# A hybrid decoder layer on one core: the input on two queues, the first modulation on TensorE, the second shift and gate on GpSimd beside sparse attention

## The chip, the cores and the metric

The kernel runs on one core of a Trainium2 chip. The metric is the device time of one execution in microseconds (us); it is given as the median of three runs. The core's engines are TensorE (PE in the rows; PEld is its weight load), VectorE (DVE), ScalarE (ACT), GpSimd (POOL) and SyncE (SP). Each takes its own stream of instructions in the order in which it stands. SyncE and ScalarE issue most of the transfers here.

## What is computed

One layer over 1024 tokens of width 1024, float32. The reference, cut to what matters for the change:

```python
mod = c_act @ w_ada[l] + b_ada[l]
sh1, sc1, ga1, sh2, sc2, ga2 = [m[:, None, :] for m in jnp.split(mod, 6, axis=-1)]
h = rmsnorm(x, g_attn[l]) * (1.0 + sc1) + sh1
proj = h @ w_in[l]
qa, ka, va, qb, ckv, qi, ki, wi = jnp.split(proj, offsets, axis=-1)
out_a = dilated_mixture(...)
ckv = rmsnorm(ckv, kv_norm_g[l])
o_lat = sparse_attention(qi.reshape(bsz, seq, IDX_HEADS, IDX_DIM), ki, wi * IDX_SCALE, q_lat, ckv, slopes_b)
out_b = jnp.einsum('bthr,hrd->bthd', o_lat, w_uv[l])
x = x + ga1 * (mixed @ w_out[l])
h2 = rmsnorm(x, g_ffn[l]) * (1.0 + sc2) + sh2
gate, up = jnp.split(h2 @ w_gu[l], 2, axis=-1)
x = x + ga2 * ((jax.nn.silu(gate) * up) @ w_down[l])
return rmsnorm(x, g_final)
```

`c_act` is one row of 1024 numbers, the silu of `c`. `w_ada` is 1024 x 6144, so that the modulation is six products of a row with a 1024 x 1024 matrix, 25 MB of weights read once. Shift 1 and scale 1 (parts 0 and 1) are needed at once, gate 1 (part 2) by w_out, scale 2 and shift 2 (parts 4 and 3) by the feed-forward's norm, gate 2 (part 5) by its last product. The keys of group B are the 256 that an indexer scores highest; that search needs the scores of all keys of a block of queries.

## The kernel before

The kernel is one program; a scheduler puts each engine's instructions into an order worked out from a simulated timeline, with the program's order as priority. Only the matmuls of the attention stages are put in a fixed order by hand (`on_pe`, L761). Results of TensorE lie in tiles with the tags `mm`, `tp` and `o`; a tag has a few buffers that are taken in turn, so that a new tile of a tag waits until the one that had its buffer has been read.

*Start.* `load_x` (L105) fetches x in two halves of four tiles of 128 tokens. Each half comes as four pieces of 32 rows (`for r in (0, 2, 1, 3)`: each piece has the tokens of one remainder by 4), 512 KB, all eight on SyncE's queue (L252). Then the weights of two index projections (`wraw`, L209) and of the first modulation follow on it (`mod1_load`, L271: 2.1 MB for each of four groups of 256 columns of shift 1 and scale 1, into `va` and `score`, which aren't in use yet). ScalarE's queue meanwhile fetches the small tensors `cc` (this is `c`) and `gst`. `norm_half` (L254) squares and scales the rows. `mod1(g)` (L277) sums one group: VectorE multiplies eight slices of weights by the column `cc[:, k]` and adds them up in `macc` (L283, L285), TensorE then sums over the partitions (L289), and the sums go into the columns `a1`, `s1`. `h_part` (L297) transposes x, applies scale and shift and splits h into a high and a low float32r part, `hh` and `hl`: every projection is three matmuls of such parts (`mm3`, L367 to L369).

*Index stretch.* `qi_proj` makes the index queries, `latent` the latent keys and the index keys, and `idx_score` (L407) for each head the products of queries and keys (TensorE, L377), a relu (ScalarE, L419), and the weighted sum (VectorE, L425). `modulation` (L328) is a generator. A step of it sums 512 columns of parts 2, 4, 3 or 5: four loads of 512 KB into `va` (L339, SyncE), eight products of TensorE with 32 columns of `cz`, in which `c` stands padded with zeros (L342), a copy, and the sum over rows (L347 for the gates, one matmul of 512 columns; L351 for the columns of `a2` and `s2`, four matmuls of one column). `mod(4)` (L472) puts four of the eight steps in front of the index scores in the program's order; the rest come in the next stage.

*Search and group A.* VectorE finds each block's top keys by bisection (`score<-...`, L622), while TensorE does the other projections; then comes group A's attention.

*Group B.* Four passes, p = 0 to 3, of two heads each. A pass has six rounds of queries, and `staged` (L732) interleaves three steps of them: `scores(r)` (kB, qB; `mm`), `turn(r)` of the round before (transposition of the softmax numerators ttB; `tp`), and `values(r)` two rounds back (`o`). The first `scores` of a pass calls `pre_b(p)` (L1036): it loads the next pass's queries (`qraw`) and has GpSimd split them into qB (L512, L513), makes the latent keys of the next pass, and in pass 1 has GpSimd multiply half of w_out by gate 1 and split it (`wo_split`, L1011: L1015, L1019, L1020, four of each on 1024 columns). The scheduler starts these splits early, in pass 0.

*After B.* x is fetched again for the residual in 32 pieces of 128 KB (L110, by `load_x` from L1089); `mixed` (L1074) loads the attention's results (`mr`), and w_out follows in two halves of four heads' pairs. Then the feed-forward, with products combined so that seven take the place of eight, follows to the end.

## Time and profile before

| | |
|---|---|
| median of 3 runs | 1443.3 us (1442.92 to 1443.64) |
| the profiled execution | 1440.91 us |
| its span in the trace | 1439.1 us |
| mean granted clock of TensorE | 0.966 |
| TensorE busy | 1290.5 us, 90% of the span |
| VectorE busy | 1055.3 us, 73% |
| ScalarE busy | 592.5 us, 41% |
| GpSimd busy | 607.6 us, 42% |
| moved by DMA | 151.58 MB, 105 GB/s on average |

The profile is of one execution. Its span runs from the first to the last instruction seen; the execution's own time is 1.8 us more, and 2.4 us under the median of the three runs. "Busy" counts the time in which an engine works on an instruction; that of issuing a transfer isn't counted. In a group of instructions the name before the arrow is written, those behind it are read; the time after "idle before" is that in which the engine stood before them, and behind it stands what it waited for.

### The profile page before, as it was taken

What the parts mean: (1) busy time and instruction counts of PE and PEld (TensorE: products, weight loads), DVE (VectorE), ACT (ScalarE), POOL (GpSimd) and SP (SyncE); (2) the same over time, 40 slices, a digit from 0 to 9 for tenths busy, and PEclk for the clock granted to TensorE, in tenths of its full rate; (3) what the DMA queues carried; (4) which work ended last, traced back from release to release, by engine and by line L of the source; (5) the groups of instructions that cost most, each with busy time, mean ns of one, the idle gap of its engine ahead of it and who ended that gap; (6) DMA issues with size and microseconds to landing.
All of it is one profiled execution on the core that took longest, in us unless ns stands there. A gap on an engine that the chain in (4) does not pass through costs nothing.

```text
span 1439.1 us, 20308 instructions
## 1 busy us (share of the span) xinstructions
PE 1290.5 (90%) x7477; PEld 1030.0 (72%) x7477; DVE 1055.3 (73%) x1808; ACT 592.5 (41%) x1203; POOL 607.6 (42%) x386
## 2 busy tenths in 40 slices
PE   0798998999978999999869999999999998988894
PEld 0675576799766777778748888888888886766773
DVE  5926699999979576745999545555545469999897
ACT  2434446564255666622653333333333223223334
POOL 2641213132243062020576544445544436487865
PEclk9999999999989999999979999999999999999998
DMA  9724523425322220353523222222223291404004
GB/s 244 217 59 149 187 89 100 142 66 132 97 80 68 67 96 16 113 160 124 168 74 102 88 88 87 67 82 87 74 88 96 91 327 36 154 22 154 0 0 117
DMA packets 132477, 151.58 MB, mean 105 GB/s; under 512 B 9429, under 2 KB 95254, under 8 KB 132378
## 3 DMA queue, kind: packets, MB, share of 16 engines
q1 hardware_dynamic: 126416, 133.23, 30.4%
q0 software_dynamic: 4672, 15.73, 3.1%
q10 hardware_dynamic: 1290, 1.32, 0.3%
q8 instruction: 59, 0.97, 0.3%
q14 instruction: 40, 0.33, 0.1%
HBM read 115.13 MB, written 34.60 MB: 104 GB/s over the span
## 4 chain that ended last, share of the span: by engine, by line
PE 56%; DVE 28%; POOL 4%; issue 4%; DMA 3%; ACT 3%; SPq 1%; DVEq 0%; ACTq 0%; POOLq 0%
DVE score L622 7%; PE mm L1220 6%; PE mm L1218 6%; PE mm L1219 6%; PE mm L367 4%; PE mm L369 4%; PE mm L368 4%; PE o L764 3%; PE mm L764 3%; PE tp L1218 3%; PE tp L1220 3%; PE tp L1219 3%; PE tp L764 2%; DVE yacc L1338 2%; DVE wo L1328 2%
## 5 line engine op out<-in xcount | busy, mean ns | idle before, releaser
L1202 ACT ACTIVATE wo<-f 128x512 fp32r<-128x512 f32 x124 | 77.8, 630 | 174.2 <-PE mm L1220 77.4
L1203 DVE TENSOR_TENSOR wo<-f,wo 128x512 fp32r<-128x512 f32 x124 | 108.3, 876 | 39.1 <-ACT wo L1202 37.2
L367 PE MATMUL mm<-hh,wl 128*128 128x512 f32 (+2 forms) x288 | 112.3, 391 | 0.1
L368 PE MATMUL mm<-hh,wh 128*128 128x512 f32 (+2 forms) x288 | 110.6, 385 | 0.0
L369 PE MATMUL mm<-hl,wh 128*128 128x512 f32 (+2 forms) x288 | 109.7, 390 | 0.0
L214 POOL TENSOR_SCALAR wh<-wraw 128x1024 fp32r<-128x1024 f32 (+1 forms) x20 | 21.2, 1078 | 116.0 <-PE mm L369 65.4
L367 PE MATMUL mm<-wo,wo 128*128 128x512 f32 x148 | 59.4, 401 | 8.1 <-DVE wo L1328 8.1
L367 PEld LDWEIGHTS mm<-hh,wl 128*128 128x128 f32 (+1 forms) x288 | 54.8, 190 | 13.9 <-issue 1.7
L369 PEld LDWEIGHTS mm<-hl,wh 128*128 128x128 f32 (+1 forms) x288 | 53.5, 189 | 15.1 <-issue 4.2
L215 POOL TENSOR_TENSOR wl<-wraw,wh 128x1024 fp32r<-128x1024 f32 (+1 forms) x22 | 53.1, 2435 | 23.7 <-ACT wh L212 23.7
L368 PEld LDWEIGHTS mm<-hh,wh 128*128 128x128 f32 (+1 forms) x288 | 54.7, 190 | 11.7 <-issue 1.1
L1015 POOL TENSOR_TENSOR wor<-wor,ga 128x1024 f32<-128x1024 f32 x8 | 19.5, 2448 | 96.2 <-DMA wor<-in_w_out_dram 94.3
L369 PE MATMUL mm<-wo,wo 128*128 128x512 f32 x148 | 57.4, 397 | 1.4 <-DVE wo L1328 1.4
L368 PE MATMUL mm<-wo,wo 128*128 128x512 f32 x148 | 58.6, 396 | 0.0
L425 DVE SCALAR_TENSOR_TENSOR score<-rl,wi,score 128x384 f32<-128x384 f32 (+2 forms) x70 | 49.7, 750 | 7.2 <-ACT rl L419 4.6
L795 ACT ACTIVATE ttB<-ttB,mn 128x128 f32<-128x128 f32 (+7 forms) x64 | 49.1, 768 | 13.6 <-DVE mn L791 13.0
L1328 DVE TENSOR_TENSOR wo<-f,wo 128x1536 fp32r<-128x1536 f32 (+1 forms) x17 | 53.6, 3155 | 0.5 <-ACT wo L1327 0.5
L1272 POOL TENSOR_TENSOR f<-f 128x512 f32<-128x512 f32 x15 | 19.4, 1293 | 79.3 <-ACT f L1271 79.3
L367 PE MATMUL mm<-wo,ml 128*128 128x512 f32 x128 | 50.7, 396 | 2.0 <-DVE ml L1079 2.0
L622 DVE TENSOR_SCALAR_CACHE_REDUCE score<-ka,sc 128x768 bf16<-128x768 int16 (+2 forms) x48 | 52.3, 1140 | 0.0
L622 DVE TENSOR_SCALAR_CACHE_REDUCE score<-kl,sc 128x1024 bf16<-128x1024 uint16 (+2 forms) x48 | 52.3, 1140 | 0.0
L369 PE MATMUL mm<-wo,mh 128*128 128x512 f32 x128 | 50.4, 393 | 0.0
(453 smaller groups left out, 4196.6 us busy)
## 6 DMA issues: line engine op xcount, KB each, us to landing
f<-in_w_gu_dram SPq DMA_DIRECT2D x44, 512.0 KB, 3.9
va<-in_w_ada_dram SPq DMA_DIRECT2D x32, 512.0 KB, 4.7
spg<-f POOLq DMA_DIRECT2D x44, 256.0 KB, 3.0
wraw<-in_w_in_dram SPq DMA_DIRECT2D x21, 512.0 KB, 4.1
f<-spg SPq DMA_DIRECT2D x33, 256.0 KB, 3.2
f<-in_w_down_dram SPq DMA_DIRECT2D x23, 256.0 KB, 3.2
more<-in_w_down_dram SPq DMA_DIRECT2D x21, 256.0 KB, 5.9
xi<-in_x_dram SPq DMA_DIRECT2D x8, 512.0 KB, 10.0
```

Of the source, the lines that this page charges most:

```text
L215: G.tensor_tensor(lo, raw, hi.bitcast(F32), op=OP.subtract)
L367: PE.matmul(p, al, bh, start=(j == 0), stop=False)
L368: PE.matmul(p, ah, bh, start=False, stop=False)
L369: PE.matmul(p, ah, bl, start=False, stop=(j == n - 1))
L622: V.tensor_scalar(mask(t, u), keys[:, seg[t]], z[:, i:i + 1], 0.0, op0=OP.is_lt, op1=OP.add, accum_out=cnt[:, i:i + 1])
L764: pe_last[0] = op(*args, **kw)
L1202: A.activation(h_, src, AF.Copy)
L1203: V.tensor_tensor(l_, src, h_.bitcast(F32), op=OP.subtract)
L1218: PE.matmul(p, w[1][:, k], a[0][:, k], start=(k == 0), stop=False)
L1219: PE.matmul(p, w[0][:, k], a[0][:, k], start=False, stop=False)
L1220: PE.matmul(p, w[0][:, k], a[1][:, k], start=False, stop=(k == 3))
L1328: V.tensor_tensor(l_, x, h_.bitcast(F32), op=OP.subtract)
```

## The change

It has four parts.

1. `load_x` takes a list of queues. x's pieces go by turns to SyncE's queue and ScalarE's, rows 0 to 31 and 32 to 63 to the first, 64 to 95 and 96 to 127 to the second. They stand ahead of the loads of `cc` and `gst` on ScalarE's queue now, and the weights of the first modulation's group 0 ahead of `wraw` on SyncE's.
2. `mod1(g)` forms its sum with eight matmuls of TensorE with the padded columns `cz` (as `modulation` does), and ScalarE copies it to `macc`.
3. `mod(4)` is gone, and `modulation` has only parts 2 and 4, four steps.
4. Parts 3 and 5 (shift 2, gate 2) are summed by `late_mod`, a half of one part in each pass of group B: four loads of 512 KB with two buffers `wlm`, eight multiplications and seven additions of 512 columns on GpSimd into the one tile `sm`, then the sum over partitions by TensorE in a `tp` tile.

```diff
-    def load_x(eng, xi, t0, t1):
+    def load_x(engs, xi, t0, t1):
-        for r in (0, 2, 1, 3):
+        for i, r in enumerate((0, 2, 1, 3)):
...
-            last = eng.dma_start(xi[32 * r:32 * r + 32], src)
+            last = engs[i % len(engs)].dma_start(xi[32 * r:32 * r + 32], src)
...
+        load_x((nc.sync, A), xh[half], half * 4, half * 4 + 4)
...
     def mod1(g):
+        p = mm_tile("o")
+        for k in range(8):
+            c0 = k % 4
+            PE.matmul(p[32 * c0:32 * c0 + 32], cz[:, k],
+                      mws[(2 * g + k // 4) % 4][:, c0].rearrange("p e n -> p (e n)"), start=(k < 4), stop=(k >= 4))
         acc = stg.tile([P, 2, 256], F32, name="macc", tag="macc", bufs=2)
-        for k in range(8):
-            w = cc[:, k:k + 1]
-            wt = mws[(2 * g + k // 4) % 4][:, k % 4]
-            if k == 0:
-                V.tensor_scalar(acc, wt, w, None, op0=OP.mult)
-            else:
-                V.scalar_tensor_tensor(acc, wt, w, acc, op0=OP.mult, op1=OP.add)
+        A.activation(acc.rearrange("p e n -> p (e n)"), p, AF.Copy)
...
-        for i in (2, 4, 3, 5):
+        for i in (2, 4):
...
-    mod(4)
     idx_score(0)
...
+    def late_mod(i, q):
+
+        o = i * D + q * 512
+        for k in range(0, 8, 2):
+            wt = at.tile([P, 2, 512], F32, name="wlm", tag="wlm", bufs=2)
+            nc.sync.dma_start(wt, wada[:, k:k + 2, o:o + 512])
+            for u in range(2):
+                G.tensor_scalar(sm if k + u == 0 else wt[:, u], wt[:, u], cc[:, k + u:k + u + 1], 1.0,
+                                op0=OP.mult, op1=OP.mult)
+                if k + u:
+                    G.tensor_tensor(sm, sm, wt[:, u], op=OP.add)
+        p = mm_tile("tp")
+        if i == 5:
+            dst = ga[:, 1, q * 512:(q + 1) * 512]
+            bb = at.tile([P, 2, 512], F32, name="wlm", tag="wlm", bufs=2)[:, 0]
+            brow = b_ada[:, o:o + 512]
+            nc.sync.dma_start(bb, bass.AP(tensor=brow.tensor, offset=brow.offset, ap=[[0, P], [1, 512]]))
+            PE.matmul(p, ones, sm, start=True, stop=True)
+            A.activation(dst, p, AF.Copy)
+            G.tensor_tensor(dst, dst, bb, op=OP.add)
+        else:
+            for k in range(4):
+                PE.matmul(p[:, k:k + 1], sm[:, k * P:(k + 1) * P], ones[:, 0:1], start=True, stop=True)
+            V.tensor_tensor(s2[:, 4 * q:4 * q + 4], p[:, :4], bcol[:, 8 * i + 4 * q:8 * i + 4 * q + 4], op=OP.add)
+
     def pre_b(p):
...
         if p == 1:
             wo_split(lambda: wor, range(4), wo0)
+        late_mod((3, 5)[p // 2], p % 2)
```

The scheduler orders the changed program anew. Three places of the two orders, with the line numbers of the kernel each belongs to:

TensorE at the start of group B's pass 0, before: the last latent product, the scores of rounds 0 and 1, then the transpositions (the numbers at the names tell the buffers).

```order
L369 MATMUL mm<-c_hl,uk_hl 128x512
L764 MATMUL mm<-kB_4348,qB_4347 128x128 x6
L764 MATMUL mm<-kB_4348,qB_4347 128x256 x6
L764 MATMUL mm<-kB_4348,qB_4347 128x384 x6
L764 MATMUL mm<-kB_4348,qB_4347 128x512 x6
L764 MATMUL tp<-ident,ttB_4799 128x128
L764 MATMUL tp<-ident,ttB_4800 128x128
```

The same place in the changed kernel:

```order
L368 MATMUL mm<-c_hl,uk_hl 128x512
L762 MATMUL mm<-kB_4278,qB_4277 128x128 x6
L762 MATMUL mm<-kB_4278,qB_4277 128x256 x6
L762 MATMUL mm<-kB_4278,qB_4277 128x384 x6
L762 MATMUL mm<-kB_4278,qB_4277 128x512 x6
L1056 MATMUL tp<-ones,sm 128x1 x4
L762 MATMUL tp<-ident,ttB_4729 128x128
L762 MATMUL tp<-ident,ttB_4730 128x128
```

The four one-column products of `late_mod` have come in between the scores of rounds 0 and 1 and the first transposition. Those of the other half of shift 2 stand ahead of pass 1's first score, and the sums of gate 2 at the start of pass 2 and early in pass 3.

GpSimd at the start of group B, before: the split of the next pass's queries, then the products and splits of w_out.

```order
L512 TENSOR_SCALAR qB_4795<-qraw 128x1024
L513 TENSOR_TENSOR qB_4795<-qraw,qB_4795 128x1024
L1015 TENSOR_TENSOR wor<-wor,ga 128x1024
L1019 TENSOR_SCALAR wo_4790<-wor 128x1024
L1020 TENSOR_TENSOR wo_4791<-wor,wo_4790 128x1024
L1015 TENSOR_TENSOR wor<-wor,ga 128x1024
```

The same place in the changed kernel:

```order
L510 TENSOR_SCALAR qB_4725<-qraw 128x1024
L511 TENSOR_TENSOR qB_4725<-qraw,qB_4725 128x1024
L1041 TENSOR_SCALAR sm<-wlm,cc 128x512
L1041 TENSOR_SCALAR wlm<-wlm,cc 128x512 x3
L1013 TENSOR_TENSOR wor<-wor,ga 128x1024
L1044 TENSOR_TENSOR sm<-sm,wlm 128x512
L1017 TENSOR_SCALAR wo_4720<-wor 128x1024
L1044 TENSOR_TENSOR sm<-sm,wlm 128x512
L1018 TENSOR_TENSOR wo_4721<-wor,wo_4720 128x1024
L1044 TENSOR_TENSOR sm<-sm,wlm 128x512
L1041 TENSOR_SCALAR wlm<-wlm,cc 128x512 x2
L1044 TENSOR_TENSOR sm<-sm,wlm 128x512
```

The sums of shift 2 stand among the splits of w_out, and go on so through both halves: 9 multiplications, 7 additions and two splits (four products and differences, two roundings) up to the first half's last addition; 17, 14 and four splits up to the second's.

SyncE's queue at the start, before:

```order
L110 DMA xi<-in_x_dram 32x4x1024 x8
L209 DMA wraw<-in_w_in_dram 128x8x128 x2
L274 DMA va<-in_w_ada_dram 128x2x256 x8
L274 DMA score<-in_w_ada_dram 128x2x256 x8
L274 DMA va<-in_w_ada_dram 128x2x256 x8
```

The same in the changed kernel:

```order
L110 DMA xi<-in_x_dram 32x4x1024 x4
L276 DMA va<-in_w_ada_dram 128x2x256 x8
L209 DMA wraw<-in_w_in_dram 128x8x128 x2
L276 DMA score<-in_w_ada_dram 128x2x256 x8
L276 DMA va<-in_w_ada_dram 128x2x256 x8
```

Four of x's eight pieces have gone to ScalarE's queue, and group 0's weights have moved ahead of `wraw`.

## Rows read from the trace of the kernel before

**Rows 1.** The page's busy time per engine over the whole span.

```profile
PE 1290.5 (90%) x7477; PEld 1030.0 (72%) x7477; DVE 1055.3 (73%) x1808; ACT 592.5 (41%) x1203; POOL 607.6 (42%) x386
```

**Rows 2.** Windows by stage; columns: PE, PEld, DVE, ACT, POOL busy, clock, DMA share, GB/s.

```profile
0.00:30.00 30.00, 0.37 (x1) 0.18 (x1) 13.84 (x45) 9.45 (x15) 5.55 (x12) 1.00 1.00 224
39.80:104.80 65.00, 59.73 (x305) 47.62 (x305) 37.48 (x60) 24.59 (x41) 30.28 (x20) 0.95 0.46 133
104.80:194.80 90.00, 82.41 (x491) 52.14 (x491) 61.91 (x98) 45.49 (x100) 19.61 (x17) 0.94 0.52 164
523.00:554.00 31.00, 29.34 (x308) 23.46 (x306) 21.95 (x69) 20.02 (x50) 18.32 (x10) 1.00 0.15 53
554.00:585.00 31.00, 29.35 (x313) 23.43 (x311) 21.98 (x73) 19.43 (x48) 0.00 (x0) 1.00 0.27 83
```

**Rows 3.** Chain of waits, 0 to 240 us: start, length, what.

```profile
2.11 11.07 DMA xi<-in_x_dram
...
69.04 1.02 PE tp L289 x8
...
142.21 3.86 DMA va<-in_w_ada_dram
...
184.60 3.81 DMA va<-in_w_ada_dram
...
208.74 3.19 DVE score L622 x6
```

**Rows 4.** Groups of VectorE, 0 to 104.8 us: busy, mean ns, then idle before.

```profile
L285 DVE SCALAR_TENSOR_TENSOR macc<-score,cc,macc 128x512 f32<-128x512 f32 x14 | 17.5, 1251 | 0.3
L285 DVE SCALAR_TENSOR_TENSOR macc<-va,cc,macc 128x512 f32<-128x512 f32 x14 | 16.5, 1181 | 0.2
```

**Rows 5.** Windows of three single stretches, columns as in rows 2.

```profile
18.00:21.00 3.00, 0.00 (x0) 0.00 (x0) 2.75 (x5) 0.00 (x0) 0.00 (x0) 1.00 1.05 214
27.00:30.00 3.00, 0.00 (x0) 0.00 (x0) 2.06 (x3) 0.76 (x2) 3.00 (x2) 1.00 1.09 348
580.00:584.00 4.00, 4.00 (x50) 3.35 (x50) 3.24 (x11) 3.02 (x6) 0.00 (x0) 1.00 0.83 260
```

**Rows 6.** Timeline of TensorE at 104 us: start, length, operation, tiles.

```profile
104.77 0.44 PE L377 MATMUL mm<-kih,qil 64*128 64x384 f32 x1
```

**Rows 7.** Groups of TensorE in the index stretch, 104.8 to 194.8 us.

```profile
L342 PE MATMUL o<-va,tab 128*32 128x512 f32 x96 | 20.4, 678 | 1.9 <-DMA va<-in_w_ada_dram 1.9
...
L351 PE MATMUL o<-ones,sm 128*128 128x1 f32 x24 | 3.1, 248 | 0.0
L347 PE MATMUL o<-sm,ones 128*128 128x512 f32 x4 | 2.2, 637 | 0.3 <-DMA sm<-in_b_ada_dram 0.3
```

**Rows 8.** Timeline of TensorE in passes 0 and 1 of group B.

```profile
501.47 1.54 PE L764 MATMUL tp<-ident,ttB 128*128 128x128 f32 x6
...
522.71 1.07 PE L764 MATMUL mm<-kB,qB 64*128 64x128 f32 x7
```

**Rows 9.** Timeline of GpSimd at the start of group B.

```profile
503.85 2.84 POOL L1015 TENSOR_TENSOR wor<-wor,ga 128x1024 f32<-128x1024 f32 x1
```

**Rows 10.** Groups of GpSimd, 480 to 640 us.

```profile
L1015 POOL TENSOR_TENSOR wor<-wor,ga 128x1024 f32<-128x1024 f32 x7 | 17.1, 2456 | 94.3 <-DMA wor<-in_w_out_dram 94.3
L1020 POOL TENSOR_TENSOR wo<-wor,wo 128x1024 fp32r<-128x1024 f32 x4 | 9.5, 2378 | 0.2
...
L1019 POOL TENSOR_SCALAR wo<-wor 128x1024 fp32r<-128x1024 f32 x4 | 4.4, 1090 | 0.3
```

**Rows 11.** Groups of GpSimd over the span: additions of 512 columns in the feed-forward.

```profile
L1244 POOL TENSOR_TENSOR f<-f 128x512 f32<-128x512 f32 x22 | 28.8, 1308 | 23.6 <-DVE wo L1203 17.6 <-DVE ml L1203 5.2 <-POOL f L1171 0.7
```

**Rows 12.** Timeline of SyncE's queue around the end of group B.

```profile
575.94 7.85 SPq L110 DMA_DIRECT2D xacc<-in_x_dram  x16
...
605.72 19.71 SPq L110 DMA_DIRECT2D f<-in_x_dram  x16
```

**Rows 13.** Timeline of VectorE in the first modulation.

```profile
31.26 0.74 DVE L285 SCALAR_TENSOR_TENSOR macc<-va,cc,macc 128x512 f32<-128x512 f32 x1
```

30 lines of the change are left out of this document (14 added, 16 removed).

## The prediction

> **What bounds the kernel now.** I read the page's busy line first: TensorE is at work for 90% of the span [rows 1], so on the whole its stream sets the time. That is a mean over stages, and the change touches three of them, so next come the windows by stage [rows 2]. In the first 30 us TensorE has done one matmul, and the stage belongs to loads and VectorE. From 39.8 to 104.8 us it is at work for 59.73 of 65 us. In the index stretch, 104.8 to 194.8 us, it has 82.41 of 90 us, VectorE 61.91. In a pass of group B (523 to 554 us) it has 29.34 of 31. Where a stage begins is read from a timeline of TensorE: the index products start at 104.77 [rows 6].
>
> The chain of waits [rows 3] says what ends last. It starts with x's load at 2.11. Within the index stretch two waits on a weight load of the modulation stand in it (3.86 and 3.81 us). From 208.74 on it is VectorE's search for the top keys. What the change does to TensorE there is worth nothing: two modulation steps stood beside the search and two still do, at 0, since VectorE's search hides them.
>
> **Start.** Removed: VectorE's 28 multiply-adds of 1.251 and 1.181 us, 14 each, 34 us [rows 4], with four first products. Added: 64 TensorE matmul records (8 fp32 products in two halves, four groups). The nearest rows are the modulation's own products of the same 32x512 shape: 96 in 20.4 us, 0.213 each [rows 7], so 13.6 us. The x load is 4.19 MB (8 of 512 KB). One queue moved its 32-row pieces at 214 GB/s in 18 to 21 us, the 128-row weight loads went at 348 in 27 to 30, and 32-row pieces of x went at 260 in group B, while other transfers ran too [rows 5]. The trace has no second queue at the start, so its price is bounded: at 214 x is in at 2.1 + 19.6 = 21.7 us, at 348 at 14.1. I take 300, between 260 and 348, as the pieces on the two queues go to different halves of the rows: 16.1. The first modulation's weights stand directly behind x now, 2.1 MB or 6.0 us at 348, plus some 3 us until they can be used: TensorE starts at about 25. If all its work then queues up, 59.73 [rows 2] + 13.6, the index products start at 98.3, 6.5 us earlier. If the loads pace it instead (x 16.1, wraw 3, four weight groups 24, landing 3, so 46 for the last group, 4 of products, and the 35.7 us that lay between the last VectorE product at 69.04 and 104.77 [rows 3, 6]), they start at 86, 19 earlier. I take **−9**, near TensorE's own bound because it was at work for 92% of that stretch; ends 0 (x no faster and TensorE as full as before) and −19.
>
> **Index stretch.** Six of eight modulation steps stood here in TensorE's stream; in the changed order gate 1's two still do. So the change does less here than its words say: 64 of 96 products go (13.6 us), the 24 one-column products (3.1 us), half of the row sums (1.1 of 2.2) [rows 7], and TensorE's waits for weights (1.9 us, same row): 19.7. What is late next is VectorE with 61.91 us [rows 2] and its score sums, so I take **−17**; ends −10 (the score chain fills the holes) and −22.
>
> **Group B, GpSimd.** Here a wait is added, and it is what decides. In the changed order TensorE's four one-column products that read the sum `sm` stand right behind the scores of the first two rounds of pass 0, ahead of every transposition of the pass. TensorE takes its stream in order, so all that stands behind waits for GpSimd: the transpositions, the value products, and through them ScalarE's and VectorE's softmax steps. Before, TensorE was at that place at 501.47 [rows 8].
>
> GpSimd begins with the sum when the query split is done, at 503.85, where its first `wor` product stood before [rows 9]. Up to the last addition of the first half the order gives it 9 multiplications and 7 additions of 512 columns, and 4 products/differences and 2 roundings of 1024 columns that split w_out. Prices: 1024-column two-operand 2456 and 2378 ns, mean 2.42 us; rounding 1.09 us [rows 10]; addition of 512 columns 1.31 us [rows 11]. No row has a multiplication of 512 columns by a scalar; 1.09 × 1.31/2.42 = 0.59, say 0.60; bounds 0.53, just under half of the 1024 row, and 1.09, that row itself. So 5.4 + 9.2 + 9.7 + 2.2 = 26.5, and 0.08 us between instructions (22 × 0.08 = 1.8): done at 532.2. **TensorE stands about 31 us.**
>
> The second half stands at the start of pass 1, ahead of its first score; TensorE was there at 522.71 [rows 8]. GpSimd needs 17 × 0.60 + 14 × 1.31 + 8 × 2.42 + 4 × 1.09 = 52.3, gaps 3.4, and I add 3 for loads, since two buffers let each 512 KB piece be asked for only when one is free and the two splits of w_out had waited for theirs too: 503.85 + 58.7 = 562.5. The first stand moves TensorE's arrival to 553.4, so 9 us more are lost: **+40** in all. Bounds: without gaps and load waits and with the cheapest multiplication +31; with the dearest (17 × 0.49 = 8 more) +47. The halves for gate 2 cost nothing: GpSimd then has a pass of 31 us for each, 8 × 0.60 + 7 × 1.31 = 14 plus a split of 3.5; that cover gone, each would cost what exceeds it. Of SyncE's queue: the loads of both first halves stand ahead of B's first store, so that store comes later, at 0, because nothing reads it before w_out.
>
> **From B to w_out.** SyncE issued 16 pieces of x at 575.94 (7.85 us), 16 more at 605.72 after the last store of B [rows 12]. Now all 32 stand behind that last store, and what w_out reads follows behind them: at most the 7.85 us and its landing, 10; at least 0, as TensorE has w_out's first products; I take **+4**.
>
> **Sum.** −9 − 17 + 40 + 4 = +18. The profiled execution took 1440.9 us (span 1439.1), 2.4 under the median of 1443.3; it gives 1458.9, and with the 2.4, **1461.3** as median.
>
> **The rivals.**
> *TensorE is not what bounds the front (0.11).* Place: 0 to 195 us. If loads and VectorE pace it and TensorE's added products fall into its stands, the start gives its −19 and the index stretch falls to VectorE's own 61.91, −28. For: TensorE does wait for weights there, 3.86 and 3.81 us in the chain. Against: it is busy for over nine tenths of both stretches. The point from which it decides is 44, the price of stand and tail: −47 + 44 = −3, 1440; with the stand at its lower end and no tail −47 + 31 = −16, 1427; middle 1434, faster than before.
>
> *The second queue brings nothing (0.23).* Then x arrives at 21.7, the weights 6 us behind, TensorE starts at about 31, and the start gives −3 in place of −9: 1467. For: the DMA engines are shown fully busy already at 214 GB/s (share 1.05, and 1.09 at 348) [rows 5]. Against: at the same share the bytes differ by the rows a piece covers, so engines wait for something that a wider set of rows relieves, and 260 was reached with 32-row pieces. The Trainium skill, "SBUF — State Buffer", section "Can I just issue two DMAs to hit both halves?", says that it can't be done: two loads at rows 0 and 64 together came to 6% more than one. By that rule x would run at some 227 GB/s and be in at 20.6 us, within a microsecond of this rival; the 260 of the row speaks against the rule, though that row has other traffic in it.
>
> *GpSimd's sums slow VectorE (0.06).* For: at the start one of VectorE's products took 0.74 us [rows 13], where their mean is 1.2 [rows 4], so something stretches such work by 1.6. A pass of B has 22 us of VectorE in 31; 1.6 times that is 35 us, 4 more than the pass, so 12 in three passes: near 1473. Against: with 18.32 us of GpSimd in one window and none in the next, VectorE has 21.95 and 21.98 us [rows 2].
>
> *It cancels (0.07).* Front −40, half way to the first rival: within 0.2%, 2.9 us, which is about what a measurement of this kernel can tell from no change.
>
> **How the numbers follow.** Forecast 0.53. The range takes in the forecast's ends as they would fall together by chance, the second and third rival, and most of the cancelling case at its low end: 1442 to 1478. Left out are the first rival below and, above, a stand at +47 with a start of 0. Faster 0.10 (the first rival, short of its upper end), same 0.07, slower 0.83.
>
> **What would show it.** In the changed profile: a stand of TensorE of 25 to 35 us just after the second score group of pass 0, released by GpSimd's `sm`, a second of some 9 us a pass later, none in passes 2 and 3; GpSimd's multiplications near 0.60 us; first index product near 96 us; VectorE's search starting near 169 us rather than 195; x's last piece in at 16. It is wrong if the stand is under 20 us, for then the front decides and the kernel may be faster; if the index stretch stays at 90 us, TensorE was not its bound and the loss is near 35.

## The result and the profile after

The changed kernel takes 1478.5 us (median of 4 runs, 1476.9 to 1480.5) against 1443.5 us of the kernel before on the same chip (4 runs, 1442.9 to 1446.1): ratio 1.024, 95% interval 1.022 to 1.026. It is slower, as forecast, but by 35 us where 18 were forecast, and the time lies half a microsecond above the range. The profiled execution has a span of 1478.0 us, 38.9 more than that of before.

Where the 38.9 us lie is read by cutting both spans at the same six events: the first index product, the first step of the top-key search, group A's first product, group B's first score, B's last value product, and the last row of `ml` that w_out reads.

| stage, us | before | after | difference | forecast |
|---|---|---|---|---|
| start, to the first index product | 104.8 | 98.8 | -6.0 | -9 |
| index stretch, to the search | 103.8 | 91.1 | -12.7 | -17 |
| search | 177.4 | 179.4 | +2.0 | 0 |
| group A | 111.1 | 115.0 | +3.9 | 0 |
| group B | 122.1 | 164.4 | +42.3 | +40 |
| from B to w_out | 87.5 | 97.8 | +10.3 | +4 |
| the rest | 732.4 | 731.5 | -0.9 | 0 |

Each column is one execution. Single executions of the kernel before lay between 1437.7 and 1453.9 us on one chip, so a difference of a few us in a stage isn't by itself beyond what executions differ by; by the medians the 38.9 are 35.0.

**Group B.** The timeline of TensorE after (start, length, operation, tiles; in brackets how long the engine stood before it and what released it):

```profile
519.19 1.87 PE L1056 MATMUL tp<-ones,sm 128*128 128x1 f32 x8 [30.95 <-POOL sm L1044]
520.92 1.57 PE L762 MATMUL tp<-ident,ttB 128*128 128x128 f32 x6
...
548.32 1.87 PE L1056 MATMUL tp<-ones,sm 128*128 128x1 f32 x8 [4.46 <-POOL sm L1044]
550.12 1.65 PE L762 MATMUL mm<-kB,qB 64*128 64x128 f32 x12
```

These are the two stands of the forecast, at the two places, with the releaser it named. Behind the first stand comes the transposition that was next in line in [rows 8]: nothing of it needs `sm`. Stands and products come to 30.95 + 1.87 + 4.46 + 1.87 = 39.2 of the 42.3 us. Of the remaining 3, some 1.6 lie between the two stands (22.8 us for what took 21.2 before) and 2.0 in the pass that follows. The windows by stage (columns as in rows 2):

```profile
0.00:30.00 30.00, 0.37 (x1) 0.18 (x1) 10.47 (x33) 9.81 (x14) 2.04 (x10) 1.00 0.99 273
34.00:98.80 64.80, 64.11 (x356) 45.30 (x352) 13.58 (x35) 27.83 (x45) 34.94 (x25) 1.00 0.49 143
98.80:188.80 90.00, 82.40 (x459) 63.38 (x459) 72.23 (x121) 45.21 (x96) 18.82 (x12) 0.92 0.24 77
519.00:550.00 31.00, 24.92 (x214) 20.47 (x214) 16.44 (x48) 13.80 (x29) 27.52 (x24) 0.89 0.38 111
550.00:581.00 31.00, 29.77 (x287) 24.54 (x289) 20.58 (x65) 18.43 (x44) 19.30 (x18) 0.92 0.35 108
```

The granted clock of 550 to 581 is 0.92 where both such windows of [rows 2] have 1.00, and that pass takes 33.0 us (550.1 to 583.1) where before it took 31.0. The lower clock stands right behind each stand: 0.51 from 519.2 to 524.2 and 0.50 from 548.3 to 553.3, against 1.00 from 524.2 to 543.8, with TensorE at work again.

GpSimd's groups, 470 to 640 us (operation, tiles, shape, count, busy us, mean ns, idle before):

```profile
L1044 POOL TENSOR_TENSOR sm<-sm,wlm 128x512 f32<-128x512 f32 x28 | 36.0, 1286 | 0.6
L1041 POOL TENSOR_SCALAR wlm<-wlm,cc 128x512 f32<-128x512 f32 x28 | 19.6, 713 | 10.9 <-DMA wlm<-in_w_ada_dram 10.9
L1018 POOL TENSOR_TENSOR wo<-wor,wo 128x1024 fp32r<-128x1024 f32 x4 | 9.5, 2367 | 0.0
L1013 POOL TENSOR_TENSOR wor<-wor,ga 128x1024 f32<-128x1024 f32 x4 | 9.4, 2352 | 1.6 <-DMA wor<-in_w_out_dram 1.6
```

The multiplication for which before had no row takes 713 ns, inside the bounds 0.53 and 1.09 and above the 0.60 taken. The first half's sum runs from 492.70 to 519.14:

```profile
492.70 0.86 POOL L1041 TENSOR_SCALAR sm<-wlm,cc 128x512 f32<-128x512 f32 x1
...
517.88 1.26 POOL L1044 TENSOR_TENSOR sm<-sm,wlm 128x512 f32<-128x512 f32 x1
```

That is 26.4 us where 28.3 were worked out (503.85 to 532.2).

**Start.** Windows of x's load, 3 to 18 us (from 7 us on the loads of the first modulation's weights are issued too):

```profile
3.00:6.00 3.00, 0.00 (x0) 0.00 (x0) 0.84 (x4) 0.00 (x0) 0.00 (x0) 1.00 1.06 305
...
15.00:18.00 3.00, 0.00 (x0) 0.00 (x0) 0.00 (x0) 0.00 (x0) 0.00 (x0) 1.00 1.06 263
```

The five windows have 305, 274, 284, 283 and 263 GB/s, at the same full DMA share as the 214 of [rows 5]. But TensorE's first product does not follow x:

```profile
31.02 3.74 PE L288 MATMUL o<-va,tab 128*32 128x512 f32 x16 [8.90 <-DMA score<-in_w_ada_dram]
```

It starts at 31.02, not at 25. The row names the weights of the next group, which land in the same moment; these products read only `va` and `tab`, the copy of `cc`. The last four of `va`'s eight loads are issued from 19.2 to 20.6 and land 3.3 to 4.6 us later, so `va` is in by about 25, as forecast. `tab` is written just before the product, at 30.8 (e6 below has it earlier, and starts at once). `cc` comes behind x on ScalarE's queue now, and its exponential behind ScalarE's squares of x. From then on TensorE has no holes: 64.11 of 64.8 us in the window 34 to 98.8, against 59.73 of 65 in [rows 2].

**Index stretch.** The chain of waits of after, in time (start, length, what):

```profile
161.90 3.19 DVE score L424 x6
...
165.61 2.92 DVE score L424 x6
...
176.56 2.80 DVE kr L571 x6
```

The modulation's weights stood in this chain in [rows 3]; now VectorE's score sums and the keys built from them (L571 to L573) end last. VectorE is at work for all of 155 to 185 us, and for 72.23 of the 90 us of the window above, against 61.91.

**From B to w_out.** SyncE's queue (issue time, length, transfer), to compare with [rows 12]:

```profile
597.44 37.69 SPq L753 DMA_DIRECT2D spm<-mxB  x4
635.22 3.63 SPq L110 DMA_DIRECT2D f<-in_x_dram  x8
638.94 19.72 SPq L110 DMA_DIRECT2D xacc<-in_x_dram  x16
658.71 3.79 SPq L110 DMA_DIRECT2D f<-in_x_dram  x8
```

All 32 pieces of x follow the last stores, as the order had it, and w_out's second half of products waits for what follows them:

```profile
675.34 0.80 PE L366 MATMUL mm<-wo,ml 128*128 128x512 f32 x1 [9.65 <-DVE ml L1103]
```

### The profile page after: what moved, and what is told of

Read it like the earlier page. It is cut to its first block, busy times and chain, and to the rows that moved or that the text cites. A ratio compares the mean times of both kernels' runs of the same rounds, so it can differ in the third digit from the quotient of the medians.

```text
span 1478.0 us, 20315 instructions
## 1 busy us (share of the span) xinstructions
PE 1294.1 (88%) x7477; PEld 1037.5 (70%) x7477; DVE 1017.0 (69%) x1778; ACT 597.4 (40%) x1203; POOL 667.0 (45%) x446
## 4 chain that ended last, share of the span: by engine, by line
PE 54%; DVE 30%; POOL 5%; DMA 5%; issue 3%; ACT 2%; SPq 1%; DVEq 0%; ACTq 0%; POOLq 0%
DVE score L620 7%; PE mm L1244 6%; PE mm L1242 5%; PE mm L1243 5%; PE mm L366 3%; PE mm L368 3%; PE mm L367 3%; PE o L762 3%; PE tp L1242 3%; PE tp L1244 3%; PE tp L1243 3%; DVE wo L1352 3%; PE mm L762 3%; PE tp L762 2%; DVE yacc L1362 2%
## 5 line engine op out<-in xcount | busy, mean ns | idle before, releaser
L1227 DVE TENSOR_TENSOR wo<-f,wo 128x512 fp32r<-128x512 f32 x124 | 101.8, 822 | 43.1 <-ACT wo L1226 40.8
L367 PE MATMUL mm<-wo,mh 128*128 128x512 f32 x128 | 51.3, 401 | 0.0
L368 PE MATMUL mm<-wo,mh 128*128 128x512 f32 x128 | 51.3, 401 | 0.0
L424 DVE SCALAR_TENSOR_TENSOR score<-rl,wi,score 128x512 f32<-128x512 f32 (+2 forms) x70 | 48.4, 748 | 3.6 <-ACT rl L418 2.6
```

The costliest lines, as they stand in the source:

```text
L367: PE.matmul(p, ah, bh, start=False, stop=False)
L368: PE.matmul(p, ah, bl, start=False, stop=(j == n - 1))
L1227: V.tensor_tensor(l_, src, h_.bitcast(F32), op=OP.subtract)
```

## The experiments

My theory after the result: the loss is TensorE's two stands and what they do to the clock, plus a tail behind x's loads; without them the front's 18.7 us would show. The rivals: GpSimd's long train of sums holds up B in any case, and x's loads are late for another reason than SyncE's queue. All stages of all runs (profiled executions, us) stand in one table; the ratio is that of the runs to those of the kernel before on the same chip. A profiled execution can lie up to 8 us from its kernel's median (e1: 1463.3 and 1470.9).

| kernel | start | index | search | A | B | to w_out | span | median | ratio, 95% interval |
|---|---|---|---|---|---|---|---|---|---|
| before | 104.8 | 103.8 | 177.4 | 111.1 | 122.1 | 87.5 | 1439.1 | | 1 |
| after | 98.8 | 91.1 | 179.4 | 115.0 | 164.4 | 97.8 | 1478.0 | 1478.5 | 1.024 (1.022 to 1.026) |
| e1_sum_last | 98.3 | 91.4 | 178.8 | 112.7 | 148.7 | 100.9 | 1461.5 | 1470.9 | 1.0162 (1.0134 to 1.0189) |
| e2_other_data | 96.7 | 91.0 | 180.3 | 117.7 | 149.2 | 99.6 | 1464.8 | 1467.7 | 1.0157 (1.0125 to 1.0188) |
| e3_c_first | 99.5 | 91.2 | 179.0 | 115.8 | 148.6 | 100.5 | 1465.1 | 1470.3 | 1.0162 (1.0139 to 1.0185) |
| e4_x_act_queue | 97.2 | 90.2 | 180.3 | 113.7 | 148.4 | 103.6 | 1464.4 | 1468.1 | 1.0162 (1.0137 to 1.0187) |
| e5_copy_on_act | 96.6 | 91.1 | 179.6 | 115.3 | 122.3 | 102.0 | 1442.5 | 1440.4 | 0.9964 (0.9943 to 0.9985) |
| e6_all_mended | 98.9 | 91.4 | 180.4 | 120.7 | 125.9 | 103.7 | 1450.0 | 1453.0 | 1.0059 (1.0038 to 1.0080) |
| e9_no_late_sums | 97.9 | 91.0 | 179.0 | 118.7 | 129.4 | 89.0 | 1437.9 | 1437.5 | 0.9946 (0.9924 to 0.9968) |
| e10_no_late_8k | 94.9 | 89.9 | 180.6 | 118.2 | 130.8 | 103.6 | 1451.1 | 1449.9 | 1.0029 (1.0015 to 1.0043) |
| e11_x_in_order | 95.9 | 90.0 | 180.4 | 113.4 | 121.5 | 107.2 | 1440.6 | 1445.5 | 0.9993 (0.9976 to 1.0010) |
| e12_x_one_queue | 99.3 | 89.5 | 178.9 | 117.4 | 130.4 | 101.4 | 1445.9 | 1451.0 | 1.0043 (1.0023 to 1.0064) |
| e13_no_added_memory | 96.7 | 90.9 | 179.7 | 118.9 | 134.4 | 87.2 | 1438.8 | 1443.0 | 0.9975 (0.9958 to 0.9992) |
| e14_before_copy | 103.2 | 104.6 | 177.5 | 112.1 | 121.1 | 87.3 | 1437.1 | 1443.0 | 0.9973 (0.9954 to 0.9992) |
| e15_mod1_on_vector | 108.5 | 92.2 | 179.6 | 115.5 | 122.2 | 102.3 | 1455.0 | 1450.4 | 1.0031 (1.0012 to 1.0050) |
| e16_own_pass | 96.9 | 91.3 | 180.2 | 113.6 | 125.0 | 88.1 | 1427.0 | 1431.2 | 0.9899 (0.9868 to 0.9931) |

### Group B: the stand, and what stood behind it

**e1_sum_last**: each half has its own tile, and TensorE reads them all behind B.

```diff
+    sms = [sm] + [at.tile([P, 512], F32, name=f"sml{j}") for j in range(3)]
...
-                    G.tensor_tensor(sm, sm, wt[:, u], op=OP.add)
+                    G.tensor_tensor(sl, sl, wt[:, u], op=OP.add)
...
+    def late_out(i, q):
...
+    for i, q in ((3, 0), (3, 1), (5, 0), (5, 1)):
+        late_out(i, q)
     atB_ctx.close()
```

> Edit: the changed kernel, but TensorE's part of the four late sums (and what follows it) stands behind the last attention product of pass 3; GpSimd's sums, their loads and their place stay, each half in a tile of its own. Theory (TensorE stands in its stream at the sum; the changed profile has 30.95 us and 4.46 us of it, released by sm): both stands go, passes 0 and 1 take 26 and 31 us again, group B is 40 to 42 us shorter, the median 1437 to 1441 us, under the kernel before. Rival (GpSimd's sums and their loads themselves slow group B): passes stay longer than 31 us with GpSimd busy, and the median stays above 1460 us.

Both stands are gone, and B falls only from 164.4 to 148.7 us. In their place TensorE stands for a key that VectorE makes (timelines of TensorE, VectorE and GpSimd):

```profile
531.33 1.61 PE L762 MATMUL mm<-kB,qB 64*128 64x256 f32 x6 [15.93 <-DVE kB L867]
```

```profile
514.44 16.23 DVE L747 COPY mxB<-rlt 128x512 f32<-128x512 f32 x1
530.60 1.27 DVE L867 TENSOR_TENSOR kB<-mm,kB 128x512 fp32r<-128x512 f32 x2
```

```profile
513.87 1.04 POOL L510 TENSOR_SCALAR qB<-qraw 128x1024 fp32r<-128x1024 f32 x1
514.88 1.26 POOL L1047 TENSOR_TENSOR sm<-sm,wlm 128x512 f32<-128x512 f32 x1
...
526.84 2.33 POOL L1018 TENSOR_TENSOR wo<-wor,wo 128x1024 fp32r<-128x1024 f32 x1
529.13 4.02 POOL L1047 TENSOR_TENSOR sml<-sml,wlm 128x512 f32<-128x512 f32 x3
```

A copy of 512 columns whose median here is 427 ns lasts 16.23 us, while GpSimd goes from one instruction to the next without a gap. My expectation fell: the stand had hidden a second cost of the same sums. Of e1's eight such copies only this one is held so long: the one at 488.29, beside the same train of GpSimd, took 0.43 us, and the greatest of the others 0.90. In e3 and e4, which have e1's edit, the copy at this place took 16.00 and 16.13. What singles it out no run shows.

These 16 us are not all of B's 26.6 us over before. In pass 0 of e1 TensorE stands once more, and VectorE's timeline has the reason:

```profile
496.27 1.12 PE L762 MATMUL tp<-ident,ttB 128*128 128x128 f32 x4 [7.13 <-ACT ptB L808]
```

```profile
491.36 2.11 DVE L1113 TENSOR_TENSOR ml<-mr,mh 128x512 fp32r<-128x512 f32 x1 [2.64 <-ACT mh L1112]
```

VectorE's order has a product `ml` of group A's results, which waits for their load, ahead of the softmax steps of round 2. Pass 0 takes 33.7 us to the first score of pass 1, where before it took 25.6. The wait is neither TensorE's reading nor the copy: e12 below, with the copy on ScalarE, has it too (6.19 us), and e9, without any sum, has part of it. How much the sums' loads lengthen it isn't shown.

**e2_other_data**: as the change, but TensorE's four products read a constant instead of `sm`, so shift 2 is left out.

```diff
-                PE.matmul(p[:, k:k + 1], sm[:, k * P:(k + 1) * P], ones[:, 0:1], start=True, stop=True)
+                PE.matmul(p[:, k:k + 1], ident, ones[:, 0:1], start=True, stop=True)
```

> Edit: the changed kernel, but TensorE's products for shift 2 read a constant tile in place of the sum, so that nothing is waited for; shift 2 is left out of the result. All of GpSimd's work and all loads stay where they were. Theory: as if the sum stood last, both stands of 31 and 4.5 us go, the median is 1437 to 1441 us. Rival (GpSimd's work slows the passes by itself): above 1460 us.

The stands for shift 2 go, and TensorE stands once, for gate 2 instead:

```profile
568.24 2.07 PE L1051 MATMUL tp<-sm,ones 128*128 128x512 f32 x2 [15.54 <-POOL sm L1044]
```

So the forecast's sentence that gate 2's halves cost nothing, as GpSimd has a pass for each, held only because the two stands had given GpSimd 39 us. VectorE's copies reach 2.3 us at most here; the wait behind `ml` in pass 0 is there again, with 5.28 us. B is 149.2 here and 148.7 in e1: with one wait removed, another of some 16 us takes its place.

**e5_copy_on_act**: e1, and ScalarE makes that broadcast copy in place of VectorE.

```diff
-            V.tensor_copy(rb, rl[:, :, :, None].to_broadcast([P, 4, 2, HD]))
+            A.activation(rb, rl[:, :, :, None].to_broadcast([P, 4, 2, HD]), AF.Copy)
```

> Edit: e1, and the broadcast of the reciprocal sums (mxB<-rlt, 128x512, one per half pass) is made by ScalarE in place of VectorE. In e1 one such copy took 16.23 us beside GpSimd's unbroken work from 484 to 533 us, where the others take 0.43; TensorE waits 15.93 us behind it for kB. Theory (VectorE's copy can't run while GpSimd works without a gap, and takes all that is queued behind it along): no VectorE instruction of group B is over 3 us, group B falls from 148.7 to 130 to 134 us, the median falls 13 to 18 us against e1. Rival (the next VectorE instruction with operands in the same memory takes the stand over, or TensorE's wait is for GpSimd's query split): less than 5 us.

The copy (row by line: least, median, greatest ns) is never stretched, and B is back at 122.3 us, better than I expected, with GpSimd busy for 90 of them:

```profile
L747 ACT ACTIVATE mxB<-rlt x8: 621/628/631, 490.3 to 599.9; 128x512 f32<-128x512 f32 x8
```

So with TensorE's reading at the end of B and the copy on ScalarE, nothing of B's +42 is left, and these two are most of it. Not all that e5 gains over e1 is the copy's, though: in the order that the scheduler made for e5, VectorE's `ml` stands behind those softmax steps, and the 7 us in pass 0 are gone as well. e12, which differs from e5 only at the start, has them back and 130.4 us in B. The early reading with the copy on ScalarE was not run. On this the Trainium skill, page "SBUF — State Buffer", section "Who interferes with whom", says of a VectorE copy in its two-port mode and a GpSimd instruction: "Whoever issues first gets the shared pair for the whole instruction; the other fully blocks". The trace fits a block in that one copy took 38 times as long, and differs in length: 16.23 us, across a dozen GpSimd instructions, not one. Which mode the copy had, no row shows.

**e14_before_copy** is the control: the kernel before with that one line of e5.

> The kernel before with one line changed: ScalarE makes the broadcast copy in place of VectorE. It is the control for the experiments that move this copy. If the copy is only dear while GpSimd works without a gap, as I hold, it gains nothing here, since it takes 0.41 to 0.43 us in the kernel before: B 122 to 124, within 3 us of before. If moving it is a gain by itself, B falls below 120 and the time by 4 us or more, and then that much of what the mended kernels gain is not the change's.

B is 121.1 us against 122.1, the ratio 0.9973 (0.9954 to 0.9992). The copy alone gains about 0.3%, 3.2 us, at the edge of the 3 that I had allowed. So e5's 0.36% is not shown to be a gain of the change: it is what before has with the copy moved.

### The tail

**e4_x_act_queue**: e1, and x's second fetch goes to ScalarE's queue.

```diff
-    x_ins = [load_x((nc.sync,), acc[t][:, None], t, t + 1) for t in first]
+    x_ins = [load_x((A,), acc[t][:, None], t, t + 1) for t in first]
```

> Edit: e1, but x's second fetch (32 pieces, for the residual) is issued on ScalarE's queue. In the changed profile from the end of group B to the last split of mixed results 10 us are lost, as all 32 pieces stand on SyncE's queue between the last store of B and the loads of what w_out reads, and TensorE waits 9.65 us. Theory (SyncE's queue holds back those loads): the wait falls under 4 us, the median falls by 4 to 7 us against e1. Rival (the 4 MB of x occupy the transfer engines, whatever queue they stand on): within 2 us of e1.

No gain: 103.6 us to w_out, and x's pieces start on the other queue at 630.6, as late as on SyncE's. It isn't the queue that holds them.

**e11_x_in_order**: e5, with the four tiles of x that are needed first loaded ahead of the others.

```diff
+        with tc.issue_after(x_ins[3].ins) if i >= 4 else nullcontext():
+            x_ins.append(load_x((nc.sync,), acc[t][:, None], t, t + 1))
```

> Edit: e5, and of x's second fetch the four tiles that w_out's first products are added to are loaded ahead of the other four (in e5 ten pieces of the others go first; VectorE waits 6.87 us for the first tile and TensorE later 10.09 us). Theory (the order of 4 MB that can only start at B's end sets the first addition): from B's end 95 to 98 us in place of 102, the median 4 to 7 us under e5. Rival (TensorE's wait is for the splits of w_out's second half, which GpSimd and ScalarE make from loads behind all of x): within 2 us of e5.

107.2 us, TensorE's longest wait for `ml` 12.7: the order among the pieces is not it either.

**e9_no_late_sums** leaves the sums of shift 2 and gate 2 out (their call goes, zeros in place of both); **e10_no_late_8k** is e9 with a tile of 8 KB per partition that nothing uses, in the pool of group B's buffers.

```diff
-        late_mod((3, 5)[p // 2], p % 2)
...
+    dmy = at.tile([P, 2048], F32, name='dmy')
```

> Edit: the changed kernel without the late sums; shift 2 and gate 2 are set to zero. It shows what the front of the change gives alone, and VectorE keeps its broadcast copies. Theory (group B's loss of 42 us and the 10 us between B and w_out come from the late sums and their memory alone): group B 122 us, to w_out 87 to 89, and with start 97, index 91, search 179, group A 113 to 116, rest 731 a span of 1420 to 1426 and a median of 1422 to 1430 us. Rival (the start's new order makes group A and what follows slower by itself): above 1436 us.

> Edit: e9, and group B's pool holds a tile of 8 KB that nobody uses, as large as the two weight buffers of the late sums. In the built order all of x's second fetch then stands behind group B's last store, as in the changed kernel, in place of half of it. Theory (the loss between B and w_out is the price of this memory: x's tiles come to lie over memory that is in use until the end of B): from B's end to the last split of mixed results 97 to 103 us, and 8 to 14 us over e9. Rival (it comes from the late sums' loads on SyncE's queue or from GpSimd): within 2 us of e9.

Nothing is computed or loaded in that tile, and the tail is 14.6 us longer (89.0, then 103.6), the median 12.3 us. SyncE's queue of e9, then of e10:

```profile
572.80 7.90 SPq L110 DMA_DIRECT2D xacc<-in_x_dram  x16
593.32 9.20 SPq L753 DMA_DIRECT2D spm<-mxB  x2
602.61 19.68 SPq L110 DMA_DIRECT2D f<-in_x_dram  x16
```

```profile
570.74 30.10 SPq L753 DMA_DIRECT2D spm<-mxB  x3
600.95 3.62 SPq L110 DMA_DIRECT2D f<-in_x_dram  x8
604.61 20.34 SPq L110 DMA_DIRECT2D xacc<-in_x_dram  x16
```

With the 8 KB, `xacc` has no place until B's buffers are given back, so its 16 pieces move from 573 us to 605, and the waits of TensorE for `ml` behind them from 1.8 us to 15.0. The change's two `wlm` buffers are these 8 KB (2 x 1024 columns x 4 bytes).

e9 also gives the price of the front alone: 7.6 us (0.9946), half of what I expected and less than the stages' -6.9 and -12.8, because group A and B come out 7.6 and 7.3 us longer than before although no sum is in them. In B 5.8 of them lie in pass 0 (31.4 us to the first score of pass 1, before 25.6), where TensorE waits 1.60 and 2.79 us for `ptB`, with VectorE's `ml` ahead of softmax steps as in e1.

### The start

**e3_c_first**: e1 with `cc` loaded ahead of x.

```diff
-    load_half(1)
-    load_half(0)
     cc = const.tile([P, 8], F32, name="cc")
     A.dma_start(cc, c.rearrange("b (p k) -> (b p) k", k=8))
+    load_half(1)
+    load_half(0)
```

> Edit: e1, and the load of c stands ahead of x's pieces on ScalarE's queue, so that its exponential is done before the squares of x. In the changed profile TensorE's first product of the first modulation starts at 31.02 us, right behind the padded column of c (30.82), though ScalarE had x's first half only at 19. Theory (the exponential's place, behind the squares and two table loads, holds TensorE): the first product moves to 23 to 27 us, when the first group's weights are in, and the median falls by 4 to 7 us against e1. Rival (the weights of the first group bound it, the profile names a wait on them): under 1 us.

No gain. `tab` is there at 24.65 now, but the first product still starts at 31.64, because the `o` tile it writes is still to be read by VectorE's copy of the columns, and that stands behind the squares of x (timeline of VectorE):

```profile
24.48 0.17 DVE L281 COPY tab<-cc 128x8 f32<-128x8 f32 x1
...
31.34 0.24 DVE L245 COPY cols<-o 128x80 f32<-128x80 f32 x1
```

**e6_all_mended**: e5 with `cc` first, the columns' tile taken from `tp`, and the sums' weights in buffers that exist (`ukr`, `uvr`), read at the end of each pass.

```diff
-    pg = mm_tile("o")
+    pg = mm_tile("tp")
...
-            wt = at.tile([P, 2, 512], F32, name="wlm", tag="wlm", bufs=2)
+            wt = wl2[k % 2]
```

> Edit: the changed kernel with late sums in the one tile sm, their weights in two tiles of 2 KB that group B does not use (so that no memory is added and the first sum can start in group A), TensorE's part at each pass's end, the next sum behind it; the broadcast copy on ScalarE as in e5; c loaded ahead of x; and the transposed small parameters in a tp tile, so that the first modulation's first product does not wait for VectorE to read the one o tile (in e3 it started 0.06 us after that copy, at 31.64). Theory, by stages of the traces: start 94 (5 less than 98.8), index 91, search 179, group A 114, group B 123 to 126, to w_out 90 to 98, rest 731: median 1428 to 1436 us, under the kernel before. Rival (each wait that is removed is followed by another of its size): above 1443 us.

A miss. The first product starts at 24.58, yet the index products start at 98.9, not earlier. Windows of e6:

```profile
24.00:34.00 10.00, 5.64 (x25) 2.34 (x26) 7.62 (x26) 5.69 (x10) 0.93 (x1) 0.88 1.07 324
34.00:44.00 10.00, 9.38 (x37) 3.67 (x36) 1.79 (x5) 4.07 (x7) 10.00 (x8) 0.61 0.98 311
```

From 24 to 44 us the granted clock is 0.88 and 0.61, where e5 has 1.00 from 31 on: 1.2 and 3.9 us of full clock less, most of the 6.4 us by which the first product came earlier. Two further losses stand in the table. Group A takes 120.7 us; GpSimd, whose weights had a place early, begins the sums there (40.4 us of work instead of 25.9), but e9 and e13 have 118.7 and 118.9 us without that, so that it is the cause isn't shown. And w_out is reached only after 103.7 us, although no memory is added. SyncE's queue of e6:

```profile
611.39 0.33 SPq L1041 DMA_DIRECT2D uvr<-in_w_ada_dram  x1
614.31 0.33 SPq L1054 DMA_DIRECT2D ukr<-in_b_ada_dram  x1
614.73 12.46 SPq L110 DMA_DIRECT2D xacc<-in_x_dram  x16
```

Here x's pieces stand behind the last loads of the sums, which go through two small buffers by turns until the end of B, and TensorE waits 13.73 us for `ml`. So late loads of the sums on SyncE's queue are a second way to the same tail.

**e12_x_one_queue** (e5, all of x on SyncE's queue) and **e15_mod1_on_vector** (e5, the first modulation on VectorE again) undo one part of the front each.

```diff
-        load_x((nc.sync, A), xh[half], half * 4, half * 4 + 4)
+        load_x((nc.sync,), xh[half], half * 4, half * 4 + 4)
```

> Edit: e5, with x on SyncE's queue alone at the start, as before. In the changed kernel x's 4.19 MB moved at 263 to 305 GB/s from 3 to 18 us, on one queue at 205 to 232. Theory (two queues bring x and all weights behind it about 5 us earlier): the index products start 3 to 6 us later than in e5 (96.6), the median rises as much. Rival (the padded column of c and TensorE's own work set the start, as e3 and e6 hint, where an earlier first product gave nothing): within 1.5 us of e5.

> As e5_copy_on_act (sums read at the end of the passes, copy on ScalarE), but the first modulation is summed by VectorE again, as before; x still comes over two queues. It tells what the part 'first modulation on TensorE' gives by itself. By the forecast TensorE gets 13.6 us more work at the start and nothing else changes there but that VectorE's 34 us go, so if TensorE bounds the start, undoing this makes the start shorter (90 to 95 us). If VectorE's chain bounded it (its 34 us stand ahead of the first projections, and the exponential and the column copies behind the squares don't then matter), undoing it makes the start longer, 99 to 105 us, and the kernel 2 to 8 us slower than e5. Stages behind the index stretch should not change by over 2 us either way.

The index products start at 96.6 us with both parts (e5; 94.9 to 98.8 among the kernels with the same front), 99.3 with TensorE's modulation alone, 108.5 with two queues alone, 104.8 and 103.2 with neither. So TensorE's modulation is what pays at the start, 12 us in this form, more than either theory had; by the ratios of the runs e15 is 0.67% slower than e5, some 10 us. The second queue by itself loses: `cc` then comes behind x, VectorE's sums begin at 30.46 us where before they began at 28.11, and TensorE's first product behind them starts 2.2 us later, more than half of the 3.7 between the two starts (TensorE, before and then e15):

```profile
39.87 1.87 PE L289 MATMUL tp<-ones,macc 128*128 128x1 f32 x8 [25.76 <-DVE macc L285]
```

```profile
42.07 1.86 PE L296 MATMUL tp<-ones,macc 128*128 128x1 f32 x8 [20.41 <-DVE macc L292]
```

Beside TensorE's modulation it brings some 3 us, no more than kernels with the same front differ by. e12's median is not a price of the queue, for its group B took 8 us more as well, 6.19 of them the wait behind `ml`. The bytes do come faster: from 3 to 6 us, with little but x under way, at 305 GB/s on two queues (after) and 238 on one (e12), 28% more; from 3 to 18 us, with the first weights among them, at a mean of 282 and 217. The Trainium skill, "SBUF — State Buffer", section "Can I just issue two DMAs to hit both halves?", has 6%; here the measurement differs from it.

### The change without what it costs

**e13_no_added_memory**: e5's copy, no added buffer, sums that can't begin before group B, and TensorE's part at ends of passes; **e16_own_pass** is e13 with gate 2's second half read in pass 3.

```diff
+    def pass_end(p):
+        for j in ((0,), (1,), (2, 3), ())[p]:
+            late_out(j)
+            if j < 2:
+                late_mod(j + 2)
```

```diff
-        for j in ((0,), (1,), (2, 3), ())[p]:
+        for j in (p,):
```

> All four parts of the change, but no buffer is added: the weights of shift 2 and gate 2 come through the two buffers in which the latent weights lay (free in group B, 512 columns each), the two halves of a part are summed in two tiles that are there already, TensorE takes each sum at the end of a pass, and ScalarE makes the broadcast copy in place of VectorE. A copy of c that waits for group A's last value tile keeps GpSimd from beginning in group A. My theory (the stand, the copy behind GpSimd's train and the 8 KB of buffers are all that the change costs): no stand of TensorE over 6 us in B, B 122 to 127 us, w_out 87 to 91 us, with the front as in e5 (start 96 to 99, index 91): span 1421 to 1430, 10 to 18 us under before. Rival (the tail is longer because x's loads meet late loads of weights, not because of memory): w_out 98 to 104, span 1435 to 1442, 0 to 8 us under before. Rival (GpSimd in its place holds up the feed of group B whatever TensorE waits for): B 135 or more, as slow as before or slower.

> As e13_no_added_memory, but TensorE takes the second half of gate 2 at the end of pass 3, its own, and not beside the first half at the end of pass 2. In e13, TensorE stood 7.1 us for that sum (of 134.4 us in B; up to its windows before that, 570 us, TensorE was at work for 78.4 of 84 us at full clock), and the clock in the window of that stand was 0.80 us per us. My theory (what is left of the loss in B is this stand and the clock behind it): no stand over 3 us in B, B 122 to 127 us, w_out 87 to 91, span 1426 to 1433, 6 to 13 us under before and 4 or more under e13. Rival (GpSimd's train, single loads of 256 KB and sums by turns, slows the feed in passes 0 and 1 as well): B stays at 130 or more, span 1436 to 1440, no gain over e13. Rival (the sum at the end of pass 3 holds up w_out in its place): B 123 to 126, but a wait of 5 us or more for the sum ahead of w_out's first product, w_out 95 or more.

e13 settles the tail: all the work is there, the 8 KB are not, the sums' loads end at 590.3 with x's first 16 pieces right behind them, and w_out is reached in 87.2 us. But I had put both halves of gate 2 at the end of pass 2, and TensorE stood there again:

```profile
593.80 2.07 PE L762 MATMUL tp<-tab,ones 128*128 128x512 f32 x2 [7.11 <-POOL tab L1052]
```

e16 moves that one reading, and B falls from 134.4 to 125.0 us, the span to 1427.0, as expected. Its waits of TensorE from 480 to 720 us, and x's pieces on SyncE's queue, where before had them [rows 12]:

```profile
PE tp L762 <- ACT ptB L808: 6.5, 10, 1.4
PE mm L366 <- DVE ml L1122: 1.6, 2, 1.2
```

```profile
587.12 7.28 SPq L110 DMA_DIRECT2D xacc<-in_x_dram  x16
594.50 0.84 SPq L753 DMA_DIRECT2D spm<-mxB  x2
595.39 19.50 SPq L110 DMA_DIRECT2D f<-in_x_dram  x16
```

No wait for a sum is left. e16 has all four parts of the change and is faster than the kernel before: 1431.2 us against 1447.1, ratio 0.9899 (0.9868 to 0.9931), beyond what the moved copy gives by itself (e14, 0.9973).

## Why the prediction was right and wrong

**Right: the sign and its place; its price in part by luck.** "TensorE stands about 31 us": 30.95. That it is so close is luck in part: the train took 26.4 us for 28.3, and GpSimd began it 4.5 us behind TensorE's arrival (492.70 and 488.24) for 2.4. The second stand was priced at 9 and took 4.46, with 2 x 1.87 for the products and some 3 of lower clock that weren't priced, so that B's +42.3 for +40 is a sum of misses that nearly cancel. The mechanism, the two places and the releaser held. There is no stand in passes 2 and 3, as forecast; e2 shows that this was so only behind the stands.

**Wrong: the other terms, which are why the time left the range.** Against +18 the stages give +38.9: 3 from the start, 4.3 from the index stretch, 5.9 from search and A, 2.3 from B and 6.3 from the tail, less 0.9 behind it.

- *Start, -9 taken, -6.0 measured.* The step that failed is "TensorE starts at about 25": I followed x and the weights and not the third operand, `cc`, which the change itself puts behind x on ScalarE's queue. TensorE's work was then 67.8 us rather than 59.73 + 13.6, so that the "TensorE's own bound" of 98.3 met the 98.8 by two errors against each other. And e3 and e6 show that an earlier `cc` would not have gained: the next wait, then the clock, took its place. e15 shows what TensorE's modulation itself is worth, 12 us of start in place of a wait of 20 us for VectorE's sums; the sum had this only as the earlier start at 25. (69.04, from which the other end of the range counts, is TensorE's own first sum behind VectorE's last product.)
- *Index stretch, -17 taken, -12.7 measured.* The step that failed is that VectorE, named as next, took only 2.7 us off the 19.7. All fourteen kernels with the changed modulation there have 89.5 to 92.2 us, whatever else they do; VectorE ends last there. The sign "VectorE's search starting near 169 us rather than 195" took the end of a window for the start of the search, which [rows 3] have at 208.74; it is at 189.9 now. So the other sign, a stretch that "stays at 90 us" and a loss "near 35", is no hit: up to the search the stretch fell from 103.8 to 91.1.
- *Tail, +4 taken of 0 to 10, +10.3 measured.* The step that failed is that "TensorE has w_out's first products" to cover it. That the loads stand behind the last store was read from the order; why, I didn't ask: it is 8 KB of memory (e9, e10, e13), not the queue (e4) nor the order of the pieces (e11). In e6, without that memory, the sums' own loads stand ahead of x until 614.7 and do the same.
- *Search and group A, +5.9, taken as 0.* Group A has 112.7 to 120.7 us in the kernels with the changed front. The step that failed is that group A has no term in the sum and no reason for having none; the search's 0 had one, and its +2.0 is the smaller part. GpSimd's early sums (e6, 120.7) don't explain it: in e9 no sum is there and A takes 118.7, at a granted clock of 0.74 in its second sixth (0.82 before). What links the front to A isn't settled.

**The rivals.** The first (TensorE isn't what bounds the front) was half right: in the index stretch VectorE was the bound, but the gain ended at its bound, -18.7 us for the front and not -47. The second (the queue brings nothing) fell for the bytes, +28%, and came near for the time, some 3 us. The third (GpSimd's sums slow VectorE) was right in kind, and hidden: not 1.6 times over all of VectorE's work, but one copy of 0.43 us that lasts 16. It shows only once the stand is gone, and that GpSimd holds it is argued from e5 and from the copies beside an idle GpSimd, which took 0.41 to 0.43.

## What to carry to other kernels

An engine that takes its stream in order must not be given a reading of a slow side engine's result in the middle of its work: the same sums cost 42 us read early and 3 read at the end of a pass (e16, with VectorE's copy moved and no buffer added too). When a stand is removed, look for what it hid before counting the gain; here a second wait, half as long, stood behind it, twice. And count a new buffer as a cost: 8 KB that are free by themselves can push later loads behind the point where the memory comes back, and so can loads that stand ahead of them on their queue.

## What the runs showed of the hardware that wasn't expected

- One VectorE copy within SBUF, 0.43 us by itself, lasted 16.23 us (e1; 16.00 in e3, 16.13 in e4) while GpSimd issued instruction after instruction; another beside the same train took 0.43. On ScalarE the same copy took 0.63 us each time (e5).
- With 32-row pieces of x on two queues the DMA engines moved 305 GB/s from 3 to 6 us (after), on one 238 (e12), at the same full busy share (1.06 and 1.03).
- TensorE's granted clock was 0.61 from 34 to 44 us in e6, with 5.64 us of work in the 10 us before; in e5, where it had stood until 31 us, it was 1.00 in the same window. 0.61 means the lower of its two levels, 1.2 GHz, for most of those 10 us. Why the earlier start has the lower clock isn't settled.
